# Splitting the down projection's weights by DMA in a two-layer hybrid transformer

## The chip, the cores and the metric

The kernel runs on one core of a Trainium2 chip. Its time is the device time of one execution in microseconds (us); where several executions were timed, the median stands. A profile is one execution, taken by the hardware profiler, with the start and the duration of every instruction on every engine. The engines are TensorE (PE in the profile, with its weight loads as a row PEld), VectorE (DVE), ScalarE (ACT), GpSimd (POOL) and SyncE (SP). TensorE multiplies and writes to PSUM, a small accumulation memory; VectorE and ScalarE read it there; DMAs move data between main memory and the on-chip SBUF, which holds 128 partitions.

## The reference

Two layers, each of them a mixer (dilated attention, retention and gated linear attention side by side), a layer norm, a feed-forward part with a causal depthwise convolution, and a second layer norm. The width is 1024, the sequence has 512 tokens, and the feed-forward width `D_FF` is 2816. The part that matters here is the feed-forward:

```python
def conv_glu_ffn(x, w_up, conv_w, conv_b, w_down):
    u = causal_dwconv(x @ w_up, conv_w, conv_b)
    gate, val = jnp.split(u, 2, axis=-1)
    return (jax.nn.silu(gate) * val) @ w_down

for l in range(DEPTH):
    mix = hybrid_mixer(x, w_in[l], ...)
    x = layer_norm(DEEPNORM_ALPHA * x + mix, ln1_g[l], ln1_b[l])
    ffn = conv_glu_ffn(x, w_up[l], conv_w[l], conv_b[l], w_down[l])
    x = layer_norm(DEEPNORM_ALPHA * x + ffn, ln2_g[l], ln2_b[l])
```

Everything is float32. `x @ w_down` is a product of 512 x 2816 with 2816 x 1024.

## The kernel before, in words

**Products in three parts.** TensorE multiplies in float32r, a shorter format of float32. To keep the precision, each operand is split into a leading part, hi, which is the value rounded to float32r, and a lower part, lo = value - hi. `mm3` (L202) then makes three matmuls of each product: hi by hi, hi by lo and lo by hi, all added up in PSUM.

**Weights.** All weights lie packed in main memory as a list of tiles, in the order in which they are used. A tile is up to 128 x 1024 values, 512 KB. `weight_tile` (L180 to L191) brings in one of them in three steps: a DMA on SP's queue loads the raw values into a tile `raw` (L186), ScalarE copies it into `hi`, which rounds it (L189), and VectorE subtracts (L190): `lo = raw - hi`. There are 2 buffers for `raw`, 5 for `hi` (tag whi) and 5 for `lo` (tag wlo), shared by all weights of the kernel. A buffer of hi or lo is free for the fifth next tile when TensorE has finished with the tile in it. `chunk` (L193) calls `weight_tile` for all tiles of one name.

**The feed-forward part** (L747 to L801) works in two halves, f = 0 and 1. In each, the up projection runs 11 times (j = 0 to 10): a pair of 128-column blocks, gate and value, of which each takes 8 steps of three matmuls into a PSUM buffer `acc`, of which there are three. Then the convolution evacuates it: ScalarE once (L741) and VectorE twice (L742, L743). The gated products become 11 row blocks, split into hi and lo.

Then the down projection runs twice, for h = 0 and 1, the two halves of the 1024 output columns (L791 to L801). Its weights are `down{f}_{h}`: 11 blocks of 128 x 512, packed in six tiles, five with two blocks and the last with one. That makes 6 tiles for each of 2 layers, 2 values of f and 2 of h: 48 tiles, 8 of them half size.

**The order inside the down projection** is that of `token_gemm` (L383). There are four tiles of 128 tokens, each with its sum in PSUM. A step is one weight block with one token tile, three matmuls. The first n - tail blocks go block by block, with all four token tiles on each. The last `tail` blocks go token tile by token tile, and after each of these `done` adds the sum to the residual stream on VectorE (`residual`, L379). So the tail's weights are held until the last token tile. The tail is 4, but 9 for f = 1 and h = 1 (L801), where the second layer norm follows each token tile.

**What sets the order of instructions.** The program gives each instruction a priority, here that of its place in the program, and a scheduler lays out a fixed order for every engine and queue ahead of the run, with waits where data or buffers are needed. Each engine and each queue then goes through its list in order, so an instruction that waits holds up what stands behind it on the same engine. POOL's queue has little in it: two elementwise operations of the mixer (L533, L557) and the loads of the layer norms' vectors `gb` (L717, called at L721 and L787).

Of the kernel before, what the change touches and what calls it, by code (L numbers as in the profile page):

```python
# [10 lines left out]
F32 = mybir.dt.float32  # L11
F32R = mybir.dt.float32r
I32 = mybir.dt.int32
AF = mybir.ActivationFunctionType
ALU = mybir.AluOpType
AX = mybir.AxisListType

P = 128
# [122 lines left out]
def hymba(ctx: ExitStack, tc: tile.TileContext, x, xt, wpk, prm, wal, lnv, cst, out):  # L141
    nc = tc.nc
    cp = ctx.enter_context(tc.tile_pool(name="cp", bufs=1))
    wp = ctx.enter_context(tc.tile_pool(name="wp", bufs=1))
# [9 lines left out]
    def nm(s):  # L154
        uid[0] += 1
        return f"{s}{uid[0]}"
# [18 lines left out]
    def bank():  # L175
        return ps_sm.tile([P, 512], F32, tag="sm", name=nm("bk"))
# [3 lines left out]
    def weight_tile(l, name, i, lo_engine, raw=None):  # L180

        o, nk, w = offsets[l, name][i]
        n = nk * w
        if raw is None:
            raw = wp.tile([P, 1024], F32, tag="raw", name=nm("raw"), bufs=2)[:, :n]
        nc.sync.dma_start(out=raw, in_=wpk[o:o + P * n].rearrange("(p n) -> p n", p=P))  # L186
        hi = wp.tile([P, 1024], F32R, tag="whi", name=nm("whi"), bufs=5)[:, :n]
        lo = wp.tile([P, 1024], F32R, tag="wlo", name=nm("wlo"), bufs=5)[:, :n]
        nc.scalar.copy(hi, raw)  # L189
        lo_engine.tensor_sub(lo, raw, hi.bitcast(F32))  # L190
        return [(hi[:, a:a + w], lo[:, a:a + w]) for a in range(0, n, w)]  # L191

    def chunk(l, name, lo_engine=None):  # L193
        kt = []
        for i in range(len(offsets[l, name])):
            kt += weight_tile(l, name, i, lo_engine or nc.vector)
        return kt
# [46 lines left out]
    def start():  # L244


        idle = page("yrg")
        V.memset(idle, 0.0)
        ps = side()
        for _ in range(6):  # L250
            mmul(ps[:, :256], idle[:, :P], idle[:, :256], start=True, stop=True)
        raws = [x4("xraw").rearrange("p a c -> p (a c)") for _ in range(3)]
        first = load_xt(0, raws[0][:, :1024], 2, 2)
        next(first)
        kt = weight_tile(0, "ret_qk", 0, V)
        next(first)
        kt += weight_tile(0, "ret_qk", 1, V)
        kt += weight_tile(0, "ret_qk", 2, V, raws[2][:, :2 * 272])
        next(load_xt(1, raws[0][:, 1024:], 1, 2))
        next(load_xt(2, raws[1][:, :1024]))  # L260
        nc.sync.dma_start(out=c_sb[:, :early], in_=cst[:, :early])
        next(load_xt(3, raws[1][:, 1024:]))
        nc.sync.dma_start(out=p_sb[0], in_=prm[0])
        nc.sync.dma_start(out=wa_sb[0], in_=wal[0])
        return kt
# [139 lines left out]
    for l in range(DEPTH):  # L405
# [85 lines left out]
        for t2 in range(2):  # L491
            parts = []
            for c in range(2):
                bk = bank()
                rs = slice(c * 64, c * 64 + 64)
                n = 2 if t2 == 0 or c == 0 else 1
# [18 lines left out]
        for t in range(NT):  # L515
# [23 lines left out]
            o = bank()  # L539
# [84 lines left out]
        def weighted(pr, c0):  # L624


            groups = ((0,), (1, 3), (2,))
            oT = bank()
            ready = []

            def products(js, pts):
                o = 0
                for j in js:
                    n = (NT - j) * P
                    for hh in range(2):
                        mmul(oT[hh * 64:hh * 64 + 64, j * P:], vv[:, j, c0 + hh * 64:c0 + hh * 64 + 64],  # L636
                             pts[hh][:, o:o + n], start=j == 0, stop=js == groups[-1])
                    o += n

            for js in groups:  # L640
                pts = []
                for hh in range(2):
                    bk, pt, o = bank(), page(), 0
                    for j in js:
                        for i in range(j, NT):
                            transpose(bk[:, o:o + P], pr[hh][i][:, j * P:(j + 1) * P])
                            o += P
                    A.copy(pt[:, :o], bk[:, :o])
                    pts.append(pt)
                ready.append((js, pts))  # L650
                if len(ready) > 1:
                    products(*ready.pop(0))
            products(*ready.pop(0))
            ot = page()
            A.copy(ot, oT)
            o = bank()
            for i in range(NT):
                transpose(o[:, i * P:(i + 1) * P], ot[:, i * P:(i + 1) * P])
            return o
# [16 lines left out]
        for g in range(2):  # L676
# [8 lines left out]
            for u in range(2):  # L685
# [6 lines left out]
                o = weighted(pr, p2 * P)  # L692
# [146 lines left out]
```

## Time and profile before

| | |
|---|---|
| median of 2 runs | 1256.1 us (1255.71 to 1256.48) |
| time of the profiled execution | 1255.33 us |
| its span | 1253.6 us |
| granted TensorE clock | 0.998 |
| moved by DMA | 116.01 MB, mean 93 GB/s |

How to read the lines: in the page's groups of instructions, a line such as "L190 DVE TENSOR_TENSOR wlo<-raw,whi" names the line of the kernel, the engine, the operation, and the tile written and those read; then follow the count, the busy time in us with the mean of one in ns, and the idle time of the engine just before them with what ended most of it. In the list of waits, "A <- B: t, n, m" says that A waited for B for t us in total, n times, at most m us at once. In a timeline, the first two numbers are start and duration in us, and the brackets hold the idle time before the instruction and what ended it. In the table by windows, each engine has its busy time and, in brackets, how many instructions. A DMA's issue line ends with its size and the median of the us from issue to landing.

### The profile page before, as it was taken

Reading aid. Unit: us, or ns where it says so; the run is one execution under the profiler, and the core shown is the slowest. Engines: PE = TensorE matmul, PEld = TensorE weight load, DVE = VectorE, ACT = ScalarE, POOL = GpSimd, SP = SyncE. Lnnn points to the kernel's source line nnn. Section 1 sums busy time; section 2 is a strip of 40 time slices with the busy share of each in tenths; the row PEclk is TensorE's granted clock in tenths of the full one; section 3 lists DMA queues with packets and bytes.
Section 4 is the critical chain, followed back from the end, with each engine's and each line's share of the span. In section 5 each row is a group of like instructions: output and inputs, shape, how many; then the busy total and the mean of one; then the engine's idle time right before and its main releaser. Section 6 shows DMA issues by size and latency. Waiting matters only on the chain.

```text
span 1253.6 us, 15361 instructions
## 1 busy us (share of the span) xinstructions
PE 1233.8 (98%) x6020; PEld 1004.1 (80%) x6020; DVE 786.7 (63%) x1519; ACT 453.1 (36%) x629; POOL 15.9 (1%) x26
## 2 busy tenths in 40 slices
PE   9999999999999999999999999999999999999997
PEld 7777777798888888888887777778988888888885
DVE  5677676687664356664767757767766633566646
ACT  4413445135442134442142134451444422444410
POOL 0010000000000000000000000000000000000000
PEclk9999999999999999999999999999999999999999
DMA  8402322224233332232142023232333322333221
GB/s 289 135 18 68 101 68 74 95 67 126 93 89 105 93 101 92 93 101 76 61 134 85 1 68 101 68 102 67 96 107 101 101 76 93 118 101 102 93 76 67
DMA packets 33399, 116.01 MB, mean 93 GB/s; under 512 B 3728, under 2 KB 4144, under 8 KB 33200
## 3 DMA queue, kind: packets, MB, share of 16 engines
q1 hardware_dynamic: 32176, 110.85, 28.0%
q0 software_dynamic: 1152, 4.19, 1.0%
q8 instruction: 47, 0.77, 0.3%
q14 instruction: 24, 0.20, 0.0%
HBM read 112.93 MB, written 2.10 MB: 92 GB/s over the span
## 4 chain that ended last, share of the span: by engine, by line
PE 90%; DMA 4%; DVE 3%; ACT 2%; issue 0%; SPq 0%; DVEq 0%; ACTq 0%
PE acc L205 25%; PE acc L203 25%; PE acc L204 25%; DMA raw<-in_wpk 4%; PE bk L277 3%; PE side L204 2%; PE side L203 2%; PE side L205 2%; DVE wlo L190 2%; ACT whi L189 2%; PE bk L636 2%; PE bk L606 1%; PE side L277 1%; PE bk L529 1%; PE bk L535 1%; PE bk L549 1%
## 5 line engine op out<-in xcount | busy, mean ns | idle before, releaser
L190 DVE TENSOR_TENSOR wlo<-raw,whi 128x1024 fp32r<-128x1024 f32 (+2 forms) x201 | 240.2, 1196 | 227.3 <-ACT whi L189 226.2
L189 ACT CAST whi<-raw 128x1024 fp32r<-128x1024 f32 (+2 forms) x201 | 206.2, 1026 | 342.6 <-PE side L205 133.8
L204 PE MATMUL acc<-xtl,whi 128*128 128x512 f32 (+1 forms) x768 | 288.7, 376 | 0.0
L205 PE MATMUL acc<-xth,wlo 128*128 128x512 f32 (+1 forms) x768 | 288.6, 376 | 0.0
L203 PE MATMUL acc<-xth,whi 128*128 128x512 f32 (+1 forms) x768 | 288.6, 377 | 0.0
L203 PEld LDWEIGHTS acc<-xth,whi 128*128 128x128 f32 x768 | 144.2, 188 | 27.5 <-issue 1.5
L204 PEld LDWEIGHTS acc<-xtl,whi 128*128 128x128 f32 x768 | 144.5, 188 | 26.5 <-DVE xtl L375 0.4
L205 PEld LDWEIGHTS acc<-xth,wlo 128*128 128x128 f32 x768 | 144.5, 188 | 26.3
L205 PE MATMUL acc<-whi,xtl 128*128 128x512 f32 (+1 forms) x384 | 147.8, 385 | 0.0
L203 PE MATMUL acc<-whi,xth 128*128 128x512 f32 (+1 forms) x384 | 147.2, 384 | 0.6 <-ACT whi L189 0.6
L204 PE MATMUL acc<-wlo,xth 128*128 128x512 f32 (+1 forms) x384 | 145.8, 380 | 0.7 <-DVE wlo L190 0.7
L203 PE MATMUL acc<-whi,yt 128*128 128x512 f32 x238 | 93.1, 391 | 0.0
L205 PE MATMUL acc<-whi,yt 128*128 128x512 f32 x238 | 92.9, 390 | 0.0
L204 PE MATMUL acc<-wlo,yt 128*128 128x512 f32 x238 | 92.6, 389 | 0.0
L205 PEld LDWEIGHTS acc<-whi,xtl 128*128 128x128 f32 x384 | 72.1, 188 | 15.6 <-issue 3.9
L203 PEld LDWEIGHTS acc<-whi,xth 128*128 128x128 f32 x384 | 72.3, 189 | 15.1 <-issue 3.2
L204 PEld LDWEIGHTS acc<-wlo,xth 128*128 128x128 f32 x384 | 72.2, 188 | 15.1 <-issue 2.2
L742 DVE SCALAR_TENSOR_TENSOR pg<-acc,prm,pg 128x511 f32<-128x511 f32 x86 | 64.2, 747 | 31.8 <-ACT pg L741 31.8
L741 ACT ACTIVATE pg<-acc,prm 128x512 f32<-128x512 f32 x86 | 66.9, 778 | 26.4 <-PE acc L205 26.4
L743 DVE SCALAR_TENSOR_TENSOR pg<-acc,prm,pg 128x510 f32<-128x510 f32 x86 | 64.4, 749 | 3.0
L379 DVE SCALAR_TENSOR_TENSOR x<-x,acc 128x512 f32<-128x512 f32 x38 | 26.1, 687 | 61.8 <-PE acc L205 61.8
L203 PE MATMUL acc<-whi,yrg 128*128 128x512 f32 x138 | 54.4, 394 | 0.0
(176 smaller groups left out, 1523.9 us busy)
## 6 DMA issues: line engine op xcount, KB each, us to landing
raw<-in_wpk SPq DMA_DIRECT2D x188, 512.0 KB, 3.6
gb<-in_lnv POOLq DMA_DIRECT2D x8, 512.0 KB, 4.6
x<-in_x SPq DMA_DIRECT2D x4, 512.0 KB, 5.9
raw<-in_wpk SPq DMA_DIRECT2D x8, 256.0 KB, 2.8
out<-x SPq DMA_DIRECT2D x8, 256.0 KB, 2.0
raw<-in_wpk SPq DMA_DIRECT2D x4, 408.0 KB, 3.5
xraw<-in_xt SPq DMA_DIRECT2D x3, 512.0 KB, 7.5
cst<-in_cst SPq DMA_DIRECT2D x1, 1222.0 KB, 8.6
```

The lines of the kernel that those rows point to most:

```text
L189: nc.scalar.copy(hi, raw)
L190: lo_engine.tensor_sub(lo, raw, hi.bitcast(F32))
L203: nc.tensor.matmul(ps, ah, bh, start=first, stop=False)
L204: nc.tensor.matmul(ps, ah, bl, start=False, stop=False)
L205: nc.tensor.matmul(ps, al, bh, start=False, stop=last)
L277: nc.tensor.transpose(dst, src, ident)
L379: V.scalar_tensor_tensor(out=xr, in0=xr, scalar=scale, in1=ps, op0=ALU.mult, op1=ALU.add)
L529: mmul(sc, kT, qbd, start=True, stop=True)
L636: mmul(oT[hh * 64:hh * 64 + 64, j * P:], vv[:, j, c0 + hh * 64:c0 + hh * 64 + 64], pts[hh][:, o:o + n], start=j == 0, stop=js == groups[-1])
L741: A.activation(out=u, in_=ps, func=AF.Identity, scale=w(2), bias=w(3))
L742: V.scalar_tensor_tensor(out=u[:, 1:], in0=ps[:, :S - 1], scalar=w(1), in1=u[:, 1:], op0=ALU.mult, op1=ALU.add)
L743: V.scalar_tensor_tensor(out=u[:, 2:], in0=ps[:, :S - 2], scalar=w(0), in1=u[:, 2:], op0=ALU.mult, op1=ALU.add)
```

## The change

For the tiles of the down projection alone, `weight_tile` takes another way. The raw weights are not subtracted on VectorE. ScalarE writes the negative of hi into lo, and a DMA on POOL's queue adds the raw weights, read from main memory, onto it: lo = -hi + raw. For f = 0 (names that begin with down0) the leading part itself comes by a DMA on POOL's queue that rounds float32 to float32r on its way, and no `raw` tile is used. For f = 1, `raw` is loaded on SP's queue and copied by ScalarE as before, and the same weights are read from main memory a second time by the adding DMA. The buffers are as many as before.

```diff
         o, nk, w = offsets[l, name][i]
         n = nk * w
+        if name.startswith("down"):
+            words = wpk[o:o + P * n].rearrange("(p n) -> p n", p=P)
+            hi = wp.tile([P, 1024], F32R, tag="whi", name=nm("whi"), bufs=5)[:, :n]
+            lo = wp.tile([P, 1024], F32R, tag="wlo", name=nm("wlo"), bufs=5)[:, :n]
+            if name.startswith("down0"):
+                nc.gpsimd.dma_start(out=hi, in_=words)
+            else:
+                raw = wp.tile([P, 1024], F32, tag="raw", name=nm("raw"), bufs=2)[:, :n]
+                nc.sync.dma_start(out=raw, in_=words)
+                nc.scalar.copy(hi, raw)
+            nc.scalar.activation(out=lo, in_=hi.bitcast(F32), func=AF.Identity, scale=-1.0)
+            nc.gpsimd.dma_start(out=lo, in_=words, accum_op=ALU.add)
+            return [(hi[:, a:a + w], lo[:, a:a + w]) for a in range(0, n, w)]
         if raw is None:
```

## The prediction

> **What bounds the kernel now.** I read the page's busy times first, then the chain and the waits of TensorE, then the stages of the down projection, then the moments at which weight buffers come free there.
>
> ```profile
> span 1253.6 us, 15361 instructions
> PE 1233.8 (98%) x6020; PEld 1004.1 (80%) x6020; DVE 786.7 (63%) x1519; ACT 453.1 (36%) x629; POOL 15.9 (1%) x26
> PE 90%; DMA 4%; DVE 3%; ACT 2%; issue 0%; SPq 0%; DVEq 0%; ACTq 0%
> L190 DVE TENSOR_TENSOR wlo<-raw,whi 128x1024 fp32r<-128x1024 f32 (+2 forms) x201 | 240.2, 1196 | 227.3 <-ACT whi L189 226.2
> L189 ACT CAST whi<-raw 128x1024 fp32r<-128x1024 f32 (+2 forms) x201 | 206.2, 1026 | 342.6 <-PE side L205 133.8
> ```
>
> TensorE is busy 98% of the span and holds 90% of the chain. The split that the change rebuilds (L189, L190) sits on engines that mostly wait. The waits of TensorE and of its weight loads on that split:
>
> ```profile
> PE acc L204 <- DVE wlo L190: 0.7, 1, 0.7
> PE acc L203 <- ACT whi L189: 0.6, 1, 0.6
> PEld acc L204 <- DVE wlo L190: 1.0, 2, 0.9
> PEld acc L203 <- ACT whi L189: 0.8, 1, 0.8
> ```
>
> The two PE waits fall in the first 30 us of the run, where nothing is changed. The down stages of layer 0, by window (f=0 h=0, f=0 h=1, f=1 h=0, f=1 h=1; layer 1 repeats them):
>
> ```profile
> core 0: us, PE busy (x) PEld busy (x) DVE busy (x) ACT busy (x) POOL busy (x), PEclk, DMA share, GB/s
> 386.00:416.00 30.00, 30.00 (x134) 24.66 (x133) 10.87 (x13) 6.20 (x8) 0.00 (x0) 1.00 0.23 79
> 416.00:446.00 30.00, 30.00 (x134) 24.86 (x133) 9.43 (x12) 5.89 (x6) 0.00 (x0) 1.00 0.33 97
> 565.50:595.50 30.00, 30.00 (x134) 24.66 (x133) 12.83 (x16) 6.34 (x8) 0.00 (x0) 1.00 0.23 80
> 595.50:628.00 32.50, 32.50 (x159) 27.34 (x158) 24.04 (x57) 6.12 (x9) 0.00 (x0) 1.00 0.21 65
> ```
>
> TensorE is never idle in them, at full clock. So the change has nothing to win there: it can only be hidden, or make weights late. The question is how much later a tile may come.
>
> **When buffers come free, and when tiles are needed.** whi and wlo have five buffers, so tile n+5 can start when TensorE is done with tile n. I call the six tiles of an h=1 stage e0 to e5; e5 is half a tile. Their hi copies, e2 to e5, for f=0 and then f=1:
>
> ```profile
> 413.27 1.05 ACT L189 CAST whi<-raw 128x1024 fp32r<-128x1024 f32 x1 [10.55 <-PE side L205]
> 414.63 1.05 ACT L189 CAST whi<-raw 128x1024 fp32r<-128x1024 f32 x1 [0.31 <-PE side L205]
> 419.17 1.05 ACT L189 CAST whi<-raw 128x1024 fp32r<-128x1024 f32 x1 [3.48 <-DMA raw<-in_wpk]
> 420.71 0.62 ACT L189 CAST whi<-raw 128x512 fp32r<-128x512 f32 x1 [0.49 <-PE side L205]
> ...
> 592.90 1.05 ACT L189 CAST whi<-raw 128x1024 fp32r<-128x1024 f32 x1 [10.55 <-PE side L205]
> 594.26 1.06 ACT L189 CAST whi<-raw 128x1024 fp32r<-128x1024 f32 x1 [0.31 <-PE side L205]
> 598.57 1.05 ACT L189 CAST whi<-raw 128x1024 fp32r<-128x1024 f32 x1 [3.25 <-DMA raw<-in_wpk]
> 600.34 0.62 ACT L189 CAST whi<-raw 128x512 fp32r<-128x512 f32 x1 [0.73 <-PE side L205]
> ```
>
> The pace comes from VectorE's timeline, where L379 marks the end of a token tile's sum:
>
> ```profile
> 437.03 0.69 DVE L379 SCALAR_TENSOR_TENSOR x<-x,acc 128x512 f32<-128x512 f32 x1 [3.13 <-PE acc L205]
> 439.75 0.69 DVE L379 SCALAR_TENSOR_TENSOR x<-x,acc 128x512 f32<-128x512 f32 x1 [2.03 <-PE acc L205]
> ...
> 593.99 1.23 DVE L190 TENSOR_TENSOR wlo<-raw,whi 128x1024 fp32r<-128x1024 f32 x1 [0.39 <-ACT whi L189]
> ...
> 606.46 0.69 DVE L379 SCALAR_TENSOR_TENSOR x<-x,acc 128x512 f32<-128x512 f32 x1 [4.77 <-PE acc L205]
> ```
>
> 439.75-437.03 is 2.72 us for the four tail steps of a token tile, 0.68 us a step; a full tile feeds 8 steps, 5.44 us. In f=0 h=1 the first sum ends at 436.95, after 32 steps, so the stage starts at 415.2. e2 is first used after 16 steps (426.1), e3 after 24 (431.5), e4 after 29 (434.9), e5 after 31 (436.3). In f=1 h=1 the tail is 9, the first sum ends at 606.4 after 17 steps, the start is 594.85, and e2 to e5 are wanted after 10, 12, 14 and 16 steps: 601.65, 603.0, 604.4, 605.75. From buffer to need e5 has 5.4 us there, in f=0 e2 has 12.8 us. The last stage with tail 9 is the tight place.
>
> **The change part by part.** Removed: 48 VectorE subtractions (40 full, 8 half). They lie beside a TensorE that does not wait, so they are worth nothing. Twenty-four loads leave SP and 24 hi copies leave ScalarE; 48 negations come to ScalarE. A negation costs what the copy row shows, 1.05 us (bounds 1.05 and 1.56, twice L741's 0.78 below); ScalarE is busy about 6 us of 30, so its time is hidden.
>
> New on POOL's queue are 24 rounding and 48 adding DMAs. The rows nearest to them:
>
> ```profile
> q1 hardware_dynamic: 32176, 110.85, 28.0%
> raw<-in_wpk SPq DMA_DIRECT2D x188, 512.0 KB, 3.6
> gb<-in_lnv POOLq DMA_DIRECT2D x8, 512.0 KB, 4.6
> xraw<-in_xt SPq DMA_DIRECT2D x3, 512.0 KB, 7.5
> L717 POOL DMA_DIRECT2D gb<-in_lnv x8: 530/530/722, 145.4 to 829.3; - x8
> ```
>
> 28.0% of 1253.6 us for 110.85 MB is 1.66 us of all DMA engines for a 512 KB pass. POOL's own load issues in 0.53 us and lands after 4.6 us: a fixed 2.9 us plus one pass. I take 4.6 us for rounding (bounds 3.6 and 7.5, the quickest and slowest 512 KB rows).
>
> The adding DMA has no row. Below, it is a plain load, one pass of 1.66 us; a gain is excluded, since TensorE does not wait now. Above, it costs three passes (read the source, read the destination, write), 5.0 us. I take two, 3.3 us, because beside a plain load it has one more read of the same size; it lands after 2.9+3.3 = 6.2 us, between the gb and xraw rows. The Trainium skill, page "Collectives: The Full Stack", section "The bandwidth ceiling: the fold count and why AG ≠ RS ≠ AR", speaks against the change: an add by DMA needs two source reads on one ring, so it runs at about half the rate of a copy (its measured ratio there is 1.93). By that rule the loss would be the one worked out below; by the gb row alone it would be nothing. No trace so far shows an add.
>
> f=1 h=1. ScalarE copies e2 at 592.90 and negates it until 595.0; e3 is through at 597.1. e4's raw buffer is free after the copy (593.95), no longer after the subtraction (595.2), so it lands at 597.3 and is negated by 599.4; e5 by 601.6. The four adds leave faster than 3.3 us each, so they queue on the DMA engines: landing at 595.0+2.9+3.3 = 601.2, then 604.5, 607.8, 609.5. Needed: 601.65, 603.0, 604.4, 605.75. The worst is e5, **3.7 us late**. With one pass, each lands 4.6 us (e5 3.8) after its negation and nothing is late; with three, e5 lands at 615.4, 9.7 us late.
>
> f=0 h=1. e2's hi leaves at 413.3, lands at 417.9, is negated at 418.95; the add lands at 425.15, or 426.8 with e4's hi pass in between, **0.7 us late**; e3 to e5 follow at 430.1, 433.4 and 435.9, in time. One pass: 0. Three: e5 at 441.8, 5.5 late.
>
> The h=0 stages have their first five tiles loaded during the up projection and are covered. A rounding tile's negation waits on ScalarE for a landing, and behind it are the evacuations of the up projection:
>
> ```profile
> 375.08 0.78 ACT L741 ACTIVATE pg<-acc,prm 128x512 f32<-128x512 f32 x1
> 376.36 0.74 DVE L742 SCALAR_TENSOR_TENSOR pg<-acc,prm,pg 128x511 f32<-128x511 f32 x1
> 377.14 0.75 DVE L743 SCALAR_TENSOR_TENSOR pg<-acc,prm,pg 128x510 f32<-128x510 f32 x1
> ```
>
> An accumulator is empty 2.8 us after L741 starts and, with three of them and 5.44 us for each, wanted again after 10.9 us: 8 us of cover for a wait of at most 4.6 us. Without the cover each excess microsecond is TensorE's.
>
> The sum: (3.7+0.7) x 2 layers = 8.8 us. The profiled execution took 1255.3 us (1253.6 of span and 1.7 around it), 0.8 us under the median of the runs. 1255.3+8.8 = 1264.1, on the median's footing **1264.9 us**.
>
> **The rivals.** *Adding is slow.* If an add holds the DMA engines three passes, layer by layer 9.7+5.5 = 15.2 us are lost, 1286.4 us; four passes (6.6 us) give 15.3+11.1 by the same working, 1308.8 us. It decides from about 4.6 us of engine time for 512 KB on: there the loss is 12.6 us a layer, 2% (about what a measurement of this kernel can tell from no change). For it: with rounding's 1.66 us, 3.8 us is all that fits in a tile's 5.44 us, so a slow add never catches up. Against it: DMA engines are busy only 0.21 to 0.33 of the down stages.
>
> *POOL's queue alternates*, each rounding DMA behind the add of the tile before. Then e5's add of f=0 h=1 lands at 440.9, 4.6 late in place of 0.7: 2 x (3.7+4.6) = 16.6, 1272.7 us. For it: program order. Against it:
>
> ```profile
> 208.74 1.05 POOL L717 DMA_DIRECT2D gb<-in_lnv  x2 [62.12 <-ACT whi L189]
> 633.69 0.40 POOL L557 TENSOR_TENSOR pg<-pg,cst 128x128 f32<-128x128 f32 x1 [423.90 <-DVE s_ln L308]
> ```
>
> The load of L787, in program order after 560 us, stands at 208.74: the queue is ordered by what can start. Nor is anything else of POOL's in the way until 633.69.
>
> *All is hidden*: an add lands like gb. 1256.1 us. *A gain*: the waits on whi and wlo above end, at most 3.1 us, 1253.0 us; against it, those named by TensorE lie at the start of the run.
>
> **How the numbers follow.** Forecast 0.41, hidden 0.18, alternating 0.12, slow adds 0.28, gain 0.01. The range, 1254 to 1300 us, runs from no loss through alternation to between three and four passes; the slow case beyond 1300 (0.13) and part of the gain are left out. Slower by over 2% is the slow case and a rest of alternation with longer rounding, 0.29; faster by over 2% would need 25 us, more than the 19.8 us in which TensorE is idle at all, 0.01; within 2%, 0.70.
>
> **What would show it.** L190 falls from 201 to 153. TensorE's new waits name the adds (wlo filled by DMA), lie in f=1 h=1 of both layers, and are 3 to 4 us each; f=0 shows under 1 us. The adds land in 6 us or more when queued, POOL's issue stays near 0.5 us. Wrong: waits in the up stages (ScalarE's cover failed), landings over 8 us alone, waits in f=0 as long as in f=1 (alternation), or no wait at all.

## The result

The changed kernel takes 1277.1 us (median, 1275.5 to 1278.7) against 1256.1 us before: a ratio of 1.0162, 95% interval 1.0142 to 1.0181. It is slower by 21 us, where 8.8 us were forecast; the range of 1254 to 1300 us holds it. In its own numbering the lines of the two kernels differ: L189, L193 to L195 are the new path, and what stood at L190 to L801 before stands 13 lines further on (L203 is the subtraction, L216 to L218 are `mm3`, L392 the residual).

The page of the changed kernel, the lines that answer to those of before:

```profile
span 1273.7 us, 15417 instructions
PE 1238.6 (97%) x6020; PEld 1004.2 (79%) x6020; DVE 733.3 (58%) x1471; ACT 475.0 (37%) x653; POOL 70.7 (6%) x98
PE 53%; DMA 4%; issue 4%; DVE 2%; ACT 1%; POOL 1%; DVEq 0%; POOLq 0%; ACTq 0%; SPq 0%
L203 DVE TENSOR_TENSOR wlo<-raw,whi 128x1024 fp32r<-128x1024 f32 (+2 forms) x153 | 185.4, 1214 | 175.6 <-ACT whi L202 174.6
q0 software_dynamic: 11520, 38.80, 14.2%
wlo<-in_wpk POOLq DMA_DIRECT2D x40, 512.0 KB, 6.2
whi<-in_wpk POOLq DMA_DIRECT2D x20, 512.0 KB, 5.6
whi<-in_wpk POOLq DMA_DIRECT2D x4, 256.0 KB, 7.9
```

VectorE has 48 subtractions less (201 to 153) and 53 us less work; the span is 20.1 us longer. q0 is what goes through GpSimd. Rounding DMAs land after 5.6 us, half ones after 7.9 us, longer than the 4.6 us that the prediction took. TensorE's waits and its weight loads' waits on weights, in the changed kernel:

```profile
PE acc L217 <- DMA wlo<-in_wpk: 13.1, 10, 2.7
PEld acc L217 <- DMA wlo<-in_wpk: 18.1, 12, 3.2
```

They did not exist before, and they name the adding DMA. Where they lie is told by the windows of the four down stages of layer 0, with GpSimd's column and the share of the DMA engines filled now:

```profile
core 0: us, PE busy (x) PEld busy (x) DVE busy (x) ACT busy (x) POOL busy (x), PEclk, DMA share, GB/s
386.00:416.00 30.00, 30.00 (x134) 24.68 (x133) 4.95 (x7) 5.97 (x7) 5.71 (x8) 1.00 0.62 144
416.00:446.00 30.00, 27.16 (x119) 21.76 (x118) 4.42 (x5) 5.91 (x7) 6.53 (x9) 1.00 0.71 176
570.00:600.00 30.00, 30.00 (x133) 24.64 (x133) 7.62 (x11) 10.51 (x13) 3.82 (x6) 1.00 0.68 154
600.00:637.50 37.50, 33.61 (x158) 26.95 (x157) 20.77 (x54) 9.33 (x13) 3.25 (x4) 1.00 0.42 102
```

Both h=0 stages are whole; both h=1 stages have lost time. To split the loss I subtract the moments of the 48 residual additions (L379 before, L392 after) and take, for each stage, how much the shift grows to its last one. The same was done for every experiment below; us, layer 0 and layer 1. The h=0 stages are at 0.4 us or less in size in all of them, except f=0 in round_only (1.1 and 0.6).

| run | f=0 h=1 | f=1 h=1 |
|---|---|---|
| changed kernel | 3.7, 6.4 | 5.3, 3.6 |
| the same again (after_again) | 4.9, 4.0 | 6.9, 3.6 |
| add_only | 0.2, 0.2 | 6.3, 3.2 |
| ahead | 1.8, 1.5 | 5.8, 3.4 |
| no_add | 0.3, 0.3 | 0.2, 0.2 |
| plain_for_add | 0.3, 0.3 | 1.9, 1.1 |
| not_last | 3.1, 5.9 | 0.0, 0.0 |
| add_only_not_last | 0.2, 0.2 | 0.0, 0.0 |
| round_only | 0.2, 0.2 | 0.0, 0.0 |
| split_add | 0.2, 0.2 | 6.9, 4.0 |
| ahead_not_last | 1.8, 1.8 | 0.0, 0.0 |

Of the changed kernel's 20.1 us, f=0 h=1 holds 10.1 and f=1 h=1 8.9. About 2 us come up in the attention, before the change's stages in each layer; in the other runs that shift lies between -0.4 and 2.6 us a layer, also where the change is nearly absent, so it is not counted as the change's.

**f=0 h=1.** GpSimd's timeline in the changed kernel: L189 is a rounding DMA, L195 an add; in brackets, what it waited for.

```profile
392.73 0.87 POOL L195 DMA_DIRECT2D wlo<-in_wpk  x1 [1.91 <-ACT wlo L194]
393.28 0.87 POOL L189 DMA_DIRECT2D whi<-in_wpk  x1
400.40 0.86 POOL L195 DMA_DIRECT2D wlo<-in_wpk  x1 [6.25 <-ACT wlo L194]
400.96 0.87 POOL L189 DMA_DIRECT2D whi<-in_wpk  x1
407.95 0.86 POOL L195 DMA_DIRECT2D wlo<-in_wpk  x1 [6.12 <-ACT wlo L194]
408.50 0.88 POOL L189 DMA_DIRECT2D whi<-in_wpk  x1
416.49 0.86 POOL L195 DMA_DIRECT2D wlo<-in_wpk  x1 [7.12 <-ACT wlo L194]
417.04 1.96 POOL L189 DMA_DIRECT2D whi<-in_wpk  x3
424.76 0.88 POOL L195 DMA_DIRECT2D wlo<-in_wpk  x1 [5.77 <-ACT wlo L194]
```

This is the alternation. Each rounding DMA here has no wait of its own: it goes out at once behind the add of the tile before, and that add has waited 6 to 7 us (the first 1.91) for its own tile's rounding and negation. A link of this chain takes about 7.6 us (393.28, 400.96, 408.50) and 8.5 us for the last one (to 417.04), a tile of TensorE's work 5.44 us. So the delay grows from tile to tile, until the three roundings of e2 to e4 go out at 417.04, though the first of their buffers was free at about 414 (413.27 before, and all is 0.8 us later here). Their adds follow at 424.76 and later, and TensorE waits at e2:

```profile
430.14 0.50 PE L217 MATMUL acc<-wlo,yt 128*128 128x512 f32 x1 [2.75 <-DMA wlo<-in_wpk]
```

**f=1 h=1.** GpSimd's four adds in the changed kernel, and the matmuls of TensorE that waited for them:

```profile
599.81 0.86 POOL L195 DMA_DIRECT2D wlo<-in_wpk  x1 [10.70 <-ACT wlo L194]
601.84 0.86 POOL L195 DMA_DIRECT2D wlo<-in_wpk  x1 [1.17 <-ACT wlo L194]
604.16 0.86 POOL L195 DMA_DIRECT2D wlo<-in_wpk  x1 [1.46 <-ACT wlo L194]
608.58 0.86 POOL L195 DMA_DIRECT2D wlo<-in_wpk  x1 [3.57 <-ACT wlo L194]
```

```profile
606.80 0.50 PE L217 MATMUL acc<-wlo,yt 128*128 128x512 f32 x1 [0.40 <-DMA wlo<-in_wpk]
610.42 0.49 PE L217 MATMUL acc<-wlo,yt 128*128 128x512 f32 x1 [1.97 <-DMA wlo<-in_wpk]
613.40 0.50 PE L217 MATMUL acc<-wlo,yt 128*128 128x512 f32 x1 [1.32 <-DMA wlo<-in_wpk]
615.26 0.50 PE L217 MATMUL acc<-wlo,yt 128*128 128x512 f32 x1 [0.20 <-DMA wlo<-in_wpk]
```

The adds are issued 2.0 and 2.3 us apart, but the matmuls that need them follow each other by 3.6 and 3.0 us. So the adds, once issued, wait for one another: a queue on the DMA engines. The last is half a tile and comes after 1.9 us.

### The profile page after: what moved, and what is told of

It reads as the page before. It is cut to its first block, busy times and chain, and to the rows that moved or that the text cites. A ratio compares the mean times of both kernels' runs of the same rounds, so it can differ in the third digit from the quotient of the medians.

```text
span 1273.7 us, 15417 instructions
## 1 busy us (share of the span) xinstructions
PE 1238.6 (97%) x6020; PEld 1004.2 (79%) x6020; DVE 733.3 (58%) x1471; ACT 475.0 (37%) x653; POOL 70.7 (6%) x98
## 2 busy tenths in 40 slices
DMA packets 40312, 139.09 MB, mean 109 GB/s; under 512 B 4496, under 2 KB 4912, under 8 KB 40112
## 3 DMA queue, kind: packets, MB, share of 16 engines
q0 software_dynamic: 11520, 38.80, 14.2%
## 4 chain that ended last, share of the span: by engine, by line
PE 53%; DMA 4%; issue 4%; DVE 2%; ACT 1%; POOL 1%; DVEq 0%; POOLq 0%; ACTq 0%; SPq 0%
PE acc L217 15%; PE acc L218 15%; PE acc L216 15%; DMA raw<-in_wpk 2%; DMA wlo<-in_wpk 2%; PE bk L290 2%; PE side L217 1%; PE side L216 1%; PE side L218 1%; DVE wlo L203 1%; PE bk L649 1%; ACT whi L202 1%; PE bk L619 1%; POOL whi L189 1%; DMA whi<-in_wpk 0%
## 5 line engine op out<-in xcount | busy, mean ns | idle before, releaser
L218 PE MATMUL acc<-xth,wlo 128*128 128x512 f32 (+1 forms) x768 | 288.6, 376 | 0.0
L216 PE MATMUL acc<-xth,whi 128*128 128x512 f32 (+1 forms) x768 | 288.5, 377 | 0.0
L203 DVE TENSOR_TENSOR wlo<-raw,whi 128x1024 fp32r<-128x1024 f32 (+2 forms) x153 | 185.4, 1214 | 175.6 <-ACT whi L202 174.6
L202 ACT CAST whi<-raw 128x1024 fp32r<-128x1024 f32 (+2 forms) x153 | 158.9, 1040 | 214.5 <-DMA raw<-in_wpk 76.2
L216 PEld LDWEIGHTS acc<-xth,whi 128*128 128x128 f32 x768 | 144.2, 188 | 27.8 <-issue 1.5
L218 PEld LDWEIGHTS acc<-xth,wlo 128*128 128x128 f32 x768 | 144.5, 188 | 26.0
L218 PE MATMUL acc<-whi,xtl 128*128 128x512 f32 (+1 forms) x384 | 147.8, 385 | 0.0
L216 PE MATMUL acc<-whi,xth 128*128 128x512 f32 (+1 forms) x384 | 147.0, 383 | 0.0
L392 DVE SCALAR_TENSOR_TENSOR x<-x,acc 128x512 f32<-128x512 f32 x38 | 26.1, 686 | 134.2 <-PE acc L218 134.2
L216 PE MATMUL acc<-whi,yt 128*128 128x512 f32 x238 | 93.6, 393 | 0.0
L218 PE MATMUL acc<-whi,yt 128*128 128x512 f32 x238 | 93.4, 393 | 0.0
L218 PEld LDWEIGHTS acc<-whi,xtl 128*128 128x128 f32 x384 | 72.1, 188 | 15.7 <-issue 3.9
L216 PEld LDWEIGHTS acc<-whi,xth 128*128 128x128 f32 x384 | 72.2, 188 | 14.5 <-issue 3.2
L194 ACT ACTIVATE wlo<-whi 128x1024 fp32r<-128x1024 f32 (+1 forms) x48 | 47.4, 988 | 90.0 <-DMA whi<-in_wpk 82.9
```

Source lines behind the costliest of these rows:

```text
L194: nc.scalar.activation(out=lo, in_=hi.bitcast(F32), func=AF.Identity, scale=-1.0)
L216: nc.tensor.matmul(ps, ah, bh, start=first, stop=False)
L218: nc.tensor.matmul(ps, al, bh, start=False, stop=last)
L392: V.scalar_tensor_tensor(out=xr, in0=xr, scalar=scale, in1=ps, op0=ALU.mult, op1=ALU.add)
```

## The experiments

Each change is against the changed kernel unless said otherwise, its diff cut to the core, and times are medians beside the kernel before on the same chip.

**after_again**: the changed kernel, as it is.

> The changed kernel once more, as the base of the other runs. Theory Q (the queue): of the 20.1 us by which its profiled span's last stage is late, 9.7 us arise in f=0 h=1 (3.5 and 6.2 in the two layers), because on GpSimd's in-order queue a rounding DMA stands behind the add of the tile before, which waits for its own rounding and negation; 8.4 us (5.1 and 3.3) arise in f=1 h=1, the stage with tail 9, because four adds queue on the DMA engines; the other 2 us arise in the attention before, at raw loads that landed later, and are not the change's. Rival B (bandwidth): both losses come from DMA engines that the adds overload, whatever the order. Rival R (rounding): the rounding DMAs and the negations themselves are what is late in f=0. All three expect +18 to +21 us against the kernel before.

Measured 1273.4 against 1257.7 us: +15.7, ratio 1.0129 (1.0111 to 1.0146). That is less than the 18 to 21 us expected. Its profiled span is 18.4 us longer than that of the kernel before: its attention adds nothing this time, its h=1 stages lose 19.5 us and its h=0 stages gain 1.1. The rest of the gap is mostly the base: the kernel before took 1257.7 us on this chip in the median, and the profiled execution from which all shifts are counted took 1255.3.

**add_only**: no rounding DMA.

```diff
-            if name.startswith("down0"):
+            if False:
                 nc.gpsimd.dma_start(out=hi, in_=words)
```

> The adds are kept in all 48 tiles, but no rounding DMA: hi comes by SP's load and ScalarE's copy for f=0 too. The same bytes move. Q: GpSimd's queue holds adds alone, f=0 loses nothing (from buffer to need 12.8 us or more, the chain is two ScalarE operations of 1.05 us, 0.9 us of issue and 6.2 us of landing), f=1 loses its 8.4 us: +8 to +11 us. B: the DMA engines carry as much, +17 to +21 us. R: +8 to +11 us as with Q.

+8.1 us, 1.0068 (1.0047 to 1.0089). The f=0 loss is gone with all the bytes still moved (139.09 MB in both), so rival B, bandwidth alone, does not make it.

**ahead**: for f=0 a rounding DMA is queued ahead of the add of the tile before (`d` is the rounding DMA of the next tile, and the block queues what it holds behind that).

```diff
+                with tc.issue_after(d.ins):
                     nc.gpsimd.dma_start(out=lo, in_=words, accum_op=ALU.add)
```

> The changed kernel, with the order on GpSimd's queue alone altered for f=0: the rounding DMA of a tile stands ahead of the add of the tile before. Q: the loss of f=0 falls from 9.7 to 0 to 3 us, +9 to +13 us in all. B: nothing changes, +18 to +21 us. R: rounding lands as late as before, +17 to +21 us.

+9.8 us, 1.0079 (1.0063 to 1.0095), as Q had it. GpSimd's timeline in it, L232 rounding and L225 adding:

```profile
396.10 0.55 POOL L232 DMA_DIRECT2D whi<-in_wpk  x1 [3.56 <-PE side L246]
396.63 0.93 POOL L225 DMA_DIRECT2D wlo<-in_wpk  x1
401.54 0.55 POOL L232 DMA_DIRECT2D whi<-in_wpk  x1 [3.98 <-PE side L246]
402.07 0.92 POOL L225 DMA_DIRECT2D wlo<-in_wpk  x1
413.10 0.55 POOL L232 DMA_DIRECT2D whi<-in_wpk  x1 [10.11 <-PE side L246]
413.63 0.93 POOL L225 DMA_DIRECT2D wlo<-in_wpk  x1
```

In these rows a rounding DMA waits for TensorE to free its buffer and for nothing else, and the adds go out behind it without a wait. The 1.8 and 1.5 us of f=0 that stay come with the remedy: the add of e1 now stands behind the rounding of e2, which waits for its buffer until 413.10. It is issued at 413.63, lands after 8.0 us, and TensorE waits 1.19 us for it at 421.70.

**no_add**: no adding DMA.

```diff
-            nc.gpsimd.dma_start(out=lo, in_=words, accum_op=ALU.add)
```

> The changed kernel without the adding DMAs: lo holds the negative of hi and the raw weights are never added, the rounding DMAs and the 48 negations stay. Q: GpSimd's queue holds rounding DMAs only, which wait for buffers alone: 0 to +2 us. B: 0 to +2 us. R: f=0 stays late, +8 to +12 us. Also tells what the 48 VectorE subtractions that are gone were worth: if they were on the path, the time falls below that of before by up to 3 us.

1256.8 against 1257.7 us, 0.9999 (0.9988 to 1.0011). Rival R falls. And 48 subtractions less on VectorE, with 48 negations more on ScalarE, are worth nothing that can be measured.

**plain_for_add**: the adding DMAs as rounding DMAs.

```diff
-            nc.gpsimd.dma_start(out=lo, in_=words, accum_op=ALU.add)
+            nc.gpsimd.dma_start(out=lo, in_=words)
```

> The changed kernel with each adding DMA replaced by a rounding DMA of the same bytes into the same tile: lo holds the rounded weights in place of the difference, nothing is added. Queue and order stay. If the adds are late for the second read on the DMA engines, the loss of f=1 falls from 8.4 to 2 to 5 us, and that of f=0, which is the queue's, stays at 7 to 10: +10 to +15 us in all. If what counts is only the length of the chain through GpSimd, it stays at +17 to +21 us.

+2.4 us, 1.0023 (1.0011 to 1.0036): both expectations are missed. Rounding DMAs stand behind the second DMA of the tile before, as in the changed kernel, and f=0 loses nothing (0.3 us a layer, as in no_add). So Q falls as it was put: the order alone does no harm. The DMA lines, of the kernel before, of plain_for_add, of add_only and of no_add, say what is different:

```profile
q0 software_dynamic: 1152, 4.19, 1.0%
```

```profile
q0 software_dynamic: 11520, 38.80, 10.1%
wlo<-in_wpk POOLq DMA_DIRECT2D x40, 512.0 KB, 4.2
whi<-in_wpk POOLq DMA_DIRECT2D x20, 512.0 KB, 3.9
```

```profile
q0 software_dynamic: 8064, 27.27, 11.3%
```

```profile
q0 software_dynamic: 4608, 15.73, 4.1%
whi<-in_wpk POOLq DMA_DIRECT2D x20, 512.0 KB, 3.8
```

Before, the norm vectors alone take 1.0% of 1253.6 us, 12.5 us. Without them, 11.3% of add_only's span of 1263.4 us is 130 us for 44 tiles' worth of adds, 2.96 us each; 4.1% of no_add's 1253.7 us is 39 us for 22 tiles' worth of roundings, 1.77 us each; plain_for_add gives 1.73 us. So an add takes the engines 1.7 times as long as a rounding. Packets and megabytes are the same with adds (the changed kernel) and without (plain_for_add): the profile does not show what the longer time goes into, and that it is a second read is not shown here. With single passes, rounding lands after 3.9 us and not 5.6, and a link of the same chain takes 5.7 us, as plain_for_add's timeline of GpSimd shows:

```profile
390.98 0.53 POOL L189 DMA_DIRECT2D whi<-in_wpk  x1 [0.20 <-issue]
396.17 0.53 POOL L195 DMA_DIRECT2D wlo<-in_wpk  x1 [4.67 <-ACT wlo L194]
396.69 0.54 POOL L189 DMA_DIRECT2D whi<-in_wpk  x1
401.85 0.53 POOL L195 DMA_DIRECT2D wlo<-in_wpk  x1 [4.62 <-ACT wlo L194]
402.37 0.54 POOL L189 DMA_DIRECT2D whi<-in_wpk  x1
```

That is close to the tile's 5.44 us, and the delay hardly grows. The issue is shorter too, 0.53 us in place of 0.87; most of the 1.9 us that a link is shorter lies in the rounding's landing.

**not_last, add_only_not_last, ahead_not_last**: in not_last the tiles of f=1 h=1 take the old way; the other two do so on top of add_only and of ahead.

```diff
-        if name.startswith("down"):
+        if name.startswith("down") and name != "down1_1":
```

> The changed kernel, but the tiles of f=1 h=1 (the stage with tail 9) take the old way: copy on ScalarE, subtraction on VectorE. Q and R: the 8.4 us of that stage go, the 9.7 us of f=0 stay: +10 to +12 us. B: a part of every stage's loss goes with a quarter of the adds: +13 to +16 us.

+7.7 us, 1.0059 (1.0044 to 1.0074). The stage's loss is gone whole and f=0 keeps its own; less than expected because the changed kernel itself, measured again, was at +15.7 and not at +20.

> Adds without rounding DMAs, and none in the stage with tail 9: 36 adds are left, all in stages with 12.8 us or more from buffer to need. Q and R: 0 to +2 us, the same as before. B: +12 to +16 us (three quarters of the adds). A gain over the kernel before is expected by none.

0.0 us, 0.9999 (0.9987 to 1.0010): 36 adds cost nothing in the stages where a tile has, by the prediction's working, 12.8 us or more.

> Both remedies at once: rounding DMAs ahead of the adds in f=0, and the old way in f=1 h=1; 36 adds and 24 rounding DMAs remain. The two losses add up (ahead was +9.8 us, of which its f=1 h=1 stages held 9.2 us of the profile), so 0 to +4 us is left, from 1.5 us a layer in f=0. A gain over the kernel before is not expected, since TensorE never waited in these stages.

+1.5 us, 1.0016 (1.0006 to 1.0025). The two losses are separate and add up: the one remedy takes 5.9 us off the 15.7, the other 8.0, both together 14.2. No version here beats the kernel before; TensorE was never idle in these stages.

**round_only**: against the kernel before, hi alone comes by a rounding DMA for f=0, raw by SP's as well, lo by VectorE.

```diff
             raw = wp.tile([P, 1024], F32, tag="raw", name=nm("raw"), bufs=2)[:, :n]
             nc.sync.dma_start(out=raw, in_=words)
+            nc.gpsimd.dma_start(out=hi, in_=words)
-            nc.scalar.copy(hi, raw)
             lo_engine.tensor_sub(lo, raw, hi.bitcast(F32))
```

> Only the rounding DMAs of f=0: hi by a DMA on GpSimd's queue, raw by SP's load as well, lo by VectorE's subtraction; f=1 as in the kernel before. The same 24 rounding DMAs, no adds and no negations. Q: the queue waits for buffers only, 0 to +2 us. B: one pass more for 24 tiles, 0 to +3 us. R: rounding itself is late, +8 to +12 us.

+1.0 us, 1.0011 (1.0000 to 1.0022): rounding by itself is hidden.

**split_add**: against add_only, each add in two halves.

```diff
-            nc.gpsimd.dma_start(out=lo, in_=words, accum_op=ALU.add)
+            for a in range(0, n, w):
+                nc.gpsimd.dma_start(out=lo[:, a:a + w], in_=words[:, a:a + w], accum_op=ALU.add)
```

> As add_only (adds in all tiles, no rounding DMA, which lost 8.1 us, all of it in f=1 h=1), with each adding DMA cut into two, one for each block of 128 x 512. The bytes are the same. If the loss is the queue of adds on the DMA engines (about 3 us of them for 512 KB), the last tiles land as late as before: +6 to +10 us. If it is the time that each single add takes to land, the first block comes about 2 us earlier: +2 to +5 us.

+11.1 us, 1.0088 (1.0065 to 1.0111). That lies above both ranges; about half of the 3 us more than add_only lies in f=1 h=1 (6.9 and 4.0 against 6.3 and 3.2), the rest in the attention. The first half hardly came earlier: the half adds land after 6.7 us in the median, the whole ones of add_only after 7.1. So a smaller add is no remedy. That is what a queue on full DMA engines would give, but the run does not separate the two explanations, because the earlier half that the second one needs did not come about. That the engines' work counts rests on plain_for_add, where the f=1 h=1 losses fall from 5.3 and 3.6 to 1.9 and 1.1.

## Why the prediction was wrong, by its steps

**Right.** That TensorE bounds these stages and has nothing to win there, that subtractions gone and negations added cost nothing (no_add), that the h=0 stages are covered, and that the stage with tail 9 would lose time. There 3.7 us a layer were forecast from adds queueing on the DMA engines; 5.3 and 3.6 us were measured. The terms behind it were near: the add at 3.3 us of engine time was 2.96, its landing at 6.2 us was 6.2 in the median (7.0 for e2, by 599.81 and 606.80), its issue 0.87 us and not 0.53. That layer 1 came out at 3.6 is in part luck, since these terms err in both directions. One more was off: the prediction has e5 negated 2.2 us after e4, but e5's raw load took 6.5 us beside the adds (such a half tile took 2.8 in the median before), and its add left 4.4 us after e4's. It cost little, because the add before it was still on its way: TensorE's wait for e5 is the 0.20 us above. The Trainium skill, "Collectives: The Full Stack", section "The bandwidth ceiling: the fold count and why AG ≠ RS ≠ AR", would have an add at half the rate of a copy; here 2.96 to 1.77 us is a factor of 1.7, in the same direction and a little less.

**Wrong: f=0 h=1, 0.7 us a layer forecast, 3.7 and 6.4 measured.** Of the 20.1 us in the profile, 10.1 lie here, where the sum has 1.4; f=1 h=1 has 8.9, where the sum has 7.4. The step that failed is the one that set the alternation of GpSimd's queue aside, with a chance of 0.12, on the ground that "the queue is ordered by what can start". The queue's order is fixed ahead of the run, and in it the next rounding DMA stood behind an add that was ready later than that DMA's buffer. Why the layout chose this order no run shows; that it reckoned the add ready sooner than the chip had it is an inference. A load hoisted by 350 us does not show that neighbours a few us apart will come in the right order.

The rounding's landing was mis-sized too, 5.6 us against 4.6, which makes each link longer. The prediction's own sign of alternation, waits in f=0 as long as in f=1, is what came: 2.75 us at e2 in layer 0, 1.97 us at most in f=1 h=1.

The rival came near in its number (1272.7 us, against 1277.1 and 1273.4 measured), but in part by luck: it started from a rounding of e2 on time at 413.3 and had e5 as the one that is late. On the chip the delay grows over three links before e2, e2's rounding leaves at 417.04, and TensorE waits at e2. The rival was also put too simply: the order (ahead: 10.1 us of f=0 become 3.3) and the longer time that an add takes (plain_for_add: 0.6) are both needed, since the chain has to be slower than 5.44 us a tile.

**Not foreseen: the clock.** See the last section. In f=0 h=1 the granted clock was at half for some 3.4 us in layer 1 of the changed kernel (6.4 us lost), in layer 0 of after_again (4.9) and in layer 1 of not_last (5.9), and at 1.00 in the other layer of each (3.7, 4.0, 3.1). The drop is worth up to 1.7 us of these differences.

**Open.** In f=1 h=1 layer 0 loses more than layer 1 in every run that has adds there. Layer 0 has the next layer's loads beside them and layer 1 has none; DMA engines are busy 0.92 and 0.84 of these stretches of the changed kernel:

```profile
599.00:615.00 16.00, 12.31 (x51) 8.95 (x49) 1.38 (x2) 5.88 (x7) 3.44 (x4) 1.00 0.92 216
1231.00:1246.00 15.00, 12.56 (x53) 9.41 (x52) 1.38 (x2) 5.78 (x7) 3.46 (x4) 1.00 0.84 176
```

That these loads are the cause is only argued; it was not tried. The clock is not the cause: in the changed kernel and in ahead it stays at 1.00 in both stages. plain_for_add has the same order (1.9 and 1.1) without an add.

## What to carry to other kernels

Work taken from an engine that waits bought nothing here; ask first what its replacement does to the slack of the tile that has least of it. When two dependent steps of one tile share an in-order queue, and the next tile's first step stands behind the second of them, the pace of the queue is the latency of the whole chain, and it has to be held against the consumer's time for a tile. Price an adding DMA by what it takes from all DMA engines, and count how many come in a burst: 36 adds were free where there was time, 12 in the two stages with little slack cost 8 us.

## What the hardware showed that was not expected

In some executions TensorE's granted clock fell to half for some us after waits of about 2 us. In add_only, TensorE waits 1.81 us at 605.47, and by windows of 2 us:

```profile
604.00:606.00 2.00, 0.54 (x2) 0.46 (x3) 0.00 (x0) 0.00 (x0) 0.63 (x1) 0.94 1.08 244
606.00:608.00 2.00, 2.00 (x6) 1.16 (x4) 0.00 (x0) 0.00 (x0) 0.00 (x0) 0.50 1.02 261
608.00:610.00 2.00, 1.43 (x4) 1.06 (x4) 0.00 (x0) 0.00 (x0) 0.00 (x0) 0.50 0.95 217
610.00:612.00 2.00, 2.00 (x6) 1.51 (x6) 0.00 (x0) 0.00 (x0) 0.00 (x0) 0.50 0.00 0
612.00:614.00 2.00, 2.00 (x9) 1.64 (x8) 1.38 (x2) 0.00 (x0) 0.00 (x0) 0.85 0.00 0
```

The granted clock (third from the end) is at or near 0.50 for some 7 us, in part of which TensorE is busy throughout: six matmuls in 2 us, where the full clock makes about nine. That is up to 3.4 us lost beside the waits; the net price is less clear, since this stage lost 6.3 us here and 5.8 in ahead, where the clock stayed at 1.00. It came in f=1 h=1 of layer 0 of after_again too (3.4 us) and of split_add (1.7 us), and in the three f=0 h=1 stages named above (1.7 us each). Waits of the same length in other stages left the clock at 1.00. For the same tile, e2 of layer 0, a wait of 2.75 us left it whole in the changed kernel (430.14), and one of 2.72 us came ahead of a drop in after_again (429.41). Nor does a drop need the adds: add_only_not_last has one (1.7 us) at 826 us, in the attention, while the DMA engines are nearly idle. The Trainium skill, "TensorE: Matmul & The Clock Gate", section "Part 1: The HAM clock gate (the "warmup" mystery)", has the clock fall to half after an idle window of about 3.4 us that runs freely. These runs agree on the half, and on the same wait halving the clock in one execution and not in another; the length of the drops, 3.4 us (1.7 us lost) or twice that, fits such a window. The longest single waits ahead of the drops in the down stages were shorter than it, 1.4 to 2.7 us. That the waits cause the drops is argued from their place alone. The first three of these windows show the DMA share at 0.95 to 1.08: while the adds are in flight, the DMA engines are full.
